# Two of four feature pairs of an FFN's opening tile in three passes of rounded parts, and two other PSUM banks for the output projection's last odd tiles

## The chip, the cores and the metric

The kernel runs on one core of a Trainium2 chip. A core has TensorE (PE in the profile; PEld is its weight load), VectorE (DVE), ScalarE (ACT), GpSimd (POOL) and SyncE (SP), each with a program of its own, and 16 DMA engines. Matmuls write to PSUM, which has eight banks; all else lies in SBUF. The metric is the device time of one execution in microseconds (us), as the median of several runs.

## What is computed

One step of a decoder trunk for 512 new prompt tokens and 8 sample tokens (520 columns in all), model width 1024, all in float32: a half-step SwiGLU FFN, a mixer (a causal pooling path and a Mamba-2 state space path side by side, with an output projection back to width 1024), a second half-step FFN, and a final norm.

```python
h = x
h = h + 0.5 * _swiglu(_rms_norm(h, ffn1_norm), ffn1_w_gate, ffn1_w_up, ffn1_w_down)
m, p, c, s = _hybrid_mixer(_rms_norm(h, mix_norm), st_pool, st_conv, st_ssm, start_pos, w_in, ..., w_out)
h = h + m
h = h + 0.5 * _swiglu(_rms_norm(h, ffn2_norm), ffn2_w_gate, ffn2_w_up, ffn2_w_down)
y = _rms_norm(h, final_norm)

def _swiglu(x, wg, wu, wd):
    return (jax.nn.silu(x @ wg) * (x @ wu)) @ wd
```

## The kernel before

Activations lie with the features on the 128 partitions and the 520 tokens in the columns, so h is eight blocks (d = 0 to 7) of 128x520. The columns are worked in two halves of 260 (b = 0, 1; HB is 260), so that the result of a matmul fits a bank.

**Numbers in two parts.** Most matmuls don't take float32 operands. A value is split into a rounded part (hi, of the type float32r, made by ACT with a cast) and the rest (lo, made by DVE as value minus hi; some weights get theirs by a DMA that adds). A product of two such pairs takes three matmuls: hi x hi, hi x lo and lo x hi. mm3 (L150 to L155) issues these three in a row; mm_low_last (L157 to L165) issues the two with the high weight for all four blocks of features and then the four with the low weight. On the rows of the profile L151, L154, L155, L160 and L165 are these matmuls. A matmul with plain float32 operands is one instruction in the code and two records in the profile; L311 is the line of such.

**The FFN in tiles.** The hidden width of 2816 is 22 tiles (f = 0 to 21) of 128. Gate and up weights of a tile come by two DMAs of 512 KB into a raw buffer; there are two such pairs of buffers. Except for the opening tile, a tile is computed by seven products instead of eight: the four blocks gate/up by column half, with features in two halves, are combined by sums of weights (tile names s, room, then shi/slo for the parts) and sums of activations. These activations are the seven slots of xth (high parts) and xtl (low parts): for each pair j of feature blocks (j and j + 4), slots 0 to 2 are the values themselves (xg, scaled by the norm's weights, with four places: slots 0 to 2 and a fourth that has no slot of its own), slots 3 to 6 are sums of them (xd, by the three steps of sums4). prep_pair makes all this for one pair: three DVE sums, two ACT casts (128x780 and 128x1040) and two DVE subtractions. Products 1 and 6 of a tile accumulate in a bank of the tag A, one after the other in the same bank with an ACT copy between them (L504); the others in a pair of banks of the tag BE.

**The opening tile.** Tile 0 of the second FFN is computed with plain float32 matmuls instead, eight for each pair j, 32 in all, straight from xg and the raw weights (plain, L298 to L315), so that PE has work while DVE and ACT make the parts for the tiles behind. Its results gather in two pairs of BE banks, P_00 (gate) and P_01 (up), which ACT copies out (keep).

**The end of the mixer.** The output projection has three groups of input features (j = 0, 1, 2; wout). A call wout(j, d2) loads a weight of 512 KB, splits it, and does four tiles of twelve matmuls: d = 2 d2 and 2 d2 + 1, for both halves. DVE adds each tile to h from its bank (L1311). In the last group (j = 2), fin follows on each block of h: ACT squares it (sq), DVE adds the squares up (acc) for the norm, and ACT writes the block of xg for pair j once d is 4 or more (the order of groups below says when). This last group and the opening tile are interleaved by

```python
LAST_PLAN = "h0 h2 h1 n0 h3 n1 n2 n3"
```

where h0 to h3 are the four calls of the last group and n0 to n3 the calls fill(0) to fill(3), one for each pair of the opening tile. For j = 2, the tiles of the last group take their banks from the two of the tag ps, and those of d = 1 from the two of the tag A.

The order of instructions on an engine isn't that of the code: when the program is built, a scheduler with a model of durations orders each engine's instructions, except where the code pins them or names one behind which another must be issued (keep_in_program_order, issue_after, high_priority). On the chip each engine runs its list in that order and waits at semaphores.

**Raw buffers.** The buffers of the projection's weights and of FFN tiles are the same ones, so a load of FFN weights waits until the DVE subtraction that reads the buffer last is done. Tile 2's weights go to tile 1's buffers, tile 3's to tile 0's.

Of the kernel before, what the change touches and what calls it, by code (L numbers as in the profile page):

```python
# [10 lines left out]
F32 = mybir.dt.float32  # L11
# [6 lines left out]
P = 128  # L18
# [50 lines left out]
def tile_trunk_step(ctx: ExitStack, tc: tile.TileContext, ins: dict, outs: dict):  # L69
# [97 lines left out]
    def ws(w, k, m=P):  # L167
        return w[:, k * m : (k + 1) * m]
# [86 lines left out]
    def prep_pair(nx, cell, xg, j, name, late=None):  # L255
        xth, xtl, _, _ = nx
        xd = cell(f"xd_{name}{j}")
        last = sums4(xg, xd)

        def parts(s, t):  # L260
            return part(xth[:, j, t], xtl[:, j, t], s)

        parts(xg[:, 0:3], slice(0, 3))
        if late is not None:
            late.append(lambda: parts(xd, slice(3, 7)))
            return None
        return last.ins, *parts(xd, slice(3, 7))

    Down = namedtuple("Down", "c d")

    class Ffn:
# [15 lines left out]
        def plain_load(self, f, j=None, us=(0, 1), queue=nc.sync):  # L287
# [3 lines left out]
            for u in us:  # L291
# [4 lines left out]
                     for t in (self.raw[f][:, u], src[2 * f + u]))  # L296
                queue.dma_start(out=next(q), in_=next(q))

        def plain(self, f, xg, j, us=(0, 1), pin=False):
            for u in us:  # L300
                if (f, u) not in self.banks:
                    n = f"P{self.i}_{f}{u}"
                    if f == 1 and u == 0:
                        bs = [ps[0].tile([P, 512], F32, tag="A", bufs=2, name=f"{n}{b}") for b in range(2)]
                    else:
                        t = ps[0].tile([P, 2, 512], F32, tag="BE", bufs=2, name=n)
                        bs = [t[:, 0], t[:, 1], t]
                    self.banks[f, u] = bs
                for q in range(2):
                    for b, slot in enumerate(((0, 1), (3, 2))):  # L310
                        mm = nc.tensor.matmul(self.banks[f, u][b][:, :HB], ws(self.raw[f][:, u], j + 4 * q),  # L311
                                              xg[:, slot[q]], start=j == q == 0, stop=j == 3 and q == 1,
                                              skip_group_check=True)
                        if pin and q == b == 0:
                            tc.keep_in_program_order(mm)  # L315

        def keep(self, f, us):

# [463 lines left out]
    def fin(d, b, hs):  # L782
# [5 lines left out]
        if j >= 0 and b:  # L788
            f2[j] = scaled(cell2, "ffn2_norm", j, "f2")

    def fill(j):
        if not j:
            f2["ffn"].plain_load(0)
        f2["ffn"].plain(0, f2[j], j)
        last = j == KD // 2 - 1
        if last:
            with tc.high_priority():
                f2["ffn"].keep(0, (0,))
        f2["ends"] = prep_pair(f2["ffn"].nx, cell2, f2[j], j, "f2")
        if last:  # L800
            with tc.high_priority(), tc.issue_after(f2["ends"][1]):
                f2["copied"] = f2["ffn"].keep(0, (1,))
# [95 lines left out]
def mixer(tc, ins, outs, e):  # L898
# [393 lines left out]
    def wout(cat, j, d2, fin=None):  # L1292
# [8 lines left out]
                               else behind.get((j, d2), ()))  # L1301
        for d in (2 * d2, 2 * d2 + 1):
            for b, hs in enumerate(HALVES):
                if d != 1 or j != 2:
                    ps = bank(f"wo{j}_{d}{b}")
                else:
                    ps = e["ps"][0].tile([P, 512], F32, tag="A", bufs=2, name=f"wo{j}_{d}{b}")
                i = range((d % 2) * 4, (d % 2) * 4 + 4)
                mm_low_last(ps[:, :HB], *([ws(w, k) for k in i] for w in (wh, wl)),
                            *([cat[:, q, k, hs] for k in range(4)] for q in range(2)), True)  # L1310
                rows.append(nc.vector.tensor_tensor(out=h[:, d, hs], in0=ps[:, :HB], in1=h[:, d, hs], op=ALU.add).ins)  # L1311
                if fin is not None:
                    fin(d, b, hs)
# [179 lines left out]
```

## Time and profile before

| | us |
|---|---|
| median of 3 runs | 950.68 |
| lowest, highest | 949.75, 951.92 |
| the profiled execution's own time | 952.73 |
| its span, first to last instruction | 950.9 |

The page gives the busy time of each engine over the span and in 40 slices, the chain of work that ended last, and the costliest groups of instructions. Windows give busy times of a stretch; the timeline gives rows with start, duration, engine, line, operation, out<-in and count, and in brackets the engine's idle time ahead of it with what ended it. In this trace the out projection's last group and the opening tile lie between 576 and 614 us, and tile 1 of the second FFN up to about 624 us. Columns 128x260 are one half's width.

### The profile page before, as it was taken

The page shows a single profiled execution, that of the slowest core. Times are in us where ns is not written, and L with a number is a line of the kernel's source. Part 1 is how long each engine was busy: PE and PEld are TensorE (multiplying, and loading weights), DVE is VectorE, ACT ScalarE, POOL GpSimd, SP SyncE. Part 2 cuts the span into 40 slices and gives each one's busy share as a digit, 9 for nine tenths or more (in the row PEclk, how much of TensorE's full clock was granted, in tenths as well). Part 3 has the DMA queues.
Part 4 walks back from the last instruction along what each step waited for, and adds up shares of the span by engine and source line. Part 5 has one row for each costly group of instructions (what it writes and reads, how often), then busy time and mean ns, then how long its engine had stood idle before and what let it go on. Part 6 is the DMA issues. An engine that isn't in the chain of part 4 may idle for free. (4 is left out here: it accounts for less than half of the span.)

```text
span 950.9 us, 19685 instructions
## 1 busy us (share of the span) xinstructions
PE 941.6 (99%) x7674; PEld 923.9 (97%) x7674; DVE 851.8 (90%) x1462; ACT 635.7 (67%) x1178; POOL 152.6 (16%) x230
## 2 busy tenths in 40 slices
PE   9999999999999999999999999999999999999996
PEld 8999999999999999999999899999999999999996
DVE  6899899998988698779998998999999999999986
ACT  7777756667566465475768745777776677766764
POOL 0011100100100002146251100111112101122120
PEclk9999999999999999999999999999999999999998
DMA  7666554455553335354364443546666655767642
GB/s 212 180 164 146 148 147 140 113 135 164 134 153 97 87 96 162 91 169 150 97 179 133 140 113 117 139 120 156 164 178 175 164 147 137 172 203 181 171 158 91
DMA packets 54123, 138.36 MB, mean 146 GB/s; under 512 B 7878, under 2 KB 16006, under 8 KB 54030
## 3 DMA queue, kind: packets, MB, share of 16 engines
q1 hardware_dynamic: 40046, 104.20, 34.6%
q0 software_dynamic: 13712, 32.78, 18.6%
q8 instruction: 60, 0.98, 0.4%
q14 instruction: 33, 0.27, 0.1%
q10 hardware_dynamic: 272, 0.13, 0.0%
HBM read 129.74 MB, written 7.34 MB: 144 GB/s over the span
## 5 line engine op out<-in xcount | busy, mean ns | idle before, releaser
L504 ACT COPY ac<-A 128x260 f32<-128x260 f32 x85 | 31.7, 373 | 34.6 <-PE A L165 16.4
L433 DVE TENSOR_TENSOR s<-raw 128x1024 f32<-128x1024 f32 x39 | 47.6, 1221 | 4.0 <-DMA raw<-in_w2gu 2.5
L504 ACT COPY ac<-BE 128x260 f32<-128x260 f32 x41 | 15.5, 377 | 33.4 <-PE BE L165 17.6
L151 PE MATMUL inx<-xh_mx,whi_inx 128*128 128x260 f32 x112 | 31.8, 284 | 0.0
L154 PE MATMUL inx<-xl_mx,whi_inx 128*128 128x260 f32 x112 | 31.6, 282 | 0.0
L155 PE MATMUL inx<-xh_mx,wlo_inx 128*128 128x260 f32 x112 | 31.6, 282 | 0.0
L1033 DVE SCALAR_TENSOR_TENSOR A<-U,h,A 128x544 f32<-128x544 f32 x36 | 28.4, 789 | 1.8 <-ACT A L1031 1.4
L311 PE MATMUL P<-x,raw 128*128 128x260 f32 x128 | 29.3, 390 | 0.0
L311 PEld LDWEIGHTS P<-x,raw 128*128 128x128 f32 x128 | 24.9, 196 | 3.9
L160 PE MATMUL wo<-catg,whi_wo 128*128 128x260 f32 x192 | 27.4, 285 | 0.0
L160 PEld LDWEIGHTS wo<-catg,whi_wo 128*128 128x128 f32 x192 | 24.8, 188 | 0.2
L139 ACT CAST thi<-raw 128x1024 fp32r<-128x1024 f32 (+1 forms) x14 | 14.2, 1014 | 15.5 <-PE wo L160 4.8
L1311 DVE TENSOR_TENSOR h<-wo,h 128x260 f32<-128x260 f32 x48 | 19.2, 423 | 4.9 <-PE wo L165 4.7
L1199 ACT ACTIVATE so<-br,sxdt 128x128 f32<-128x128 f32 x64 | 22.7, 375 | 1.2 <-DVE room L1201 0.7
L252 DVE TENSOR_TENSOR gs<-gq,gs 128x780 fp32r<-128x780 f32 (+1 forms) x28 | 23.2, 829 | 0.0
L151 PE MATMUL inz<-xh_mx,whi_inz 128*128 128x260 f32 x80 | 22.9, 287 | 0.0
L154 PE MATMUL inz<-xl_mx,whi_inz 128*128 128x260 f32 x80 | 22.7, 283 | 0.0
L155 PE MATMUL inz<-xh_mx,wlo_inz 128*128 128x260 f32 x80 | 22.6, 283 | 0.0
L512 DVE TENSOR_TENSOR BE<-BE,ac 128x260 f32<-128x260 f32 (+1 forms) x41 | 18.5, 451 | 3.1 <-PE BE L155 1.7
L151 PEld LDWEIGHTS inx<-xh_mx,whi_inx 128*128 128x128 f32 x112 | 21.1, 188 | 0.2 <-issue 0.2
L160 PE MATMUL A<-xth_f,qs 128*128 128x260 f32 x84 | 21.2, 283 | 0.0
L160 PE MATMUL A<-xtl_f,qs 128*128 128x260 f32 x84 | 21.2, 284 | 0.0
(3135 smaller groups left out, 4380.9 us busy)
## 6 DMA issues: line engine op xcount, KB each, us to landing
raw<-in_w2gu SPq DMA_DIRECT2D x44, 512.0 KB, 4.3
raw<-in_w1gu SPq DMA_DIRECT2D x41, 512.0 KB, 4.2
raw<-in_w_in SPq DMA_DIRECT2D x24, 512.0 KB, 3.6
raw<-in_w1d SPq DMA_DIRECT2D x16, 512.0 KB, 4.6
raw<-in_w2d SPq DMA_DIRECT2D x16, 512.0 KB, 4.3
raw<-in_w_out SPq DMA_DIRECT2D x12, 512.0 KB, 3.5
ab<-scr_acs SPq DMA_DIRECT2D x8, 512.0 KB, 6.3
h<-in_state_ssm SPq DMA_DIRECT2D x16, 256.0 KB, 3.7
```

What stands on the lines that cost most here:

```text
L151: first = nc.tensor.matmul(ps, whi, xhi, start=start, stop=False, **kw)
L154: nc.tensor.matmul(ps, whi, xlo, start=False, stop=False, **kw)
L155: nc.tensor.matmul(ps, wlo, xhi, start=False, stop=stop, **kw)
L160: mm = nc.tensor.matmul(ps, w, x, start=start, stop=False, **kw)
L252: low = nc.vector.tensor_tensor(out=lo, in0=s, in1=hi.bitcast(F32), op=ALU.subtract)
L311: mm = nc.tensor.matmul(self.banks[f, u][b][:, :HB], ws(self.raw[f][:, u], j + 4 * q), xg[:, slot[q]], start=j == q == 0, stop=j == 3 and ...
L433: nc.vector.tensor_tensor(out=s1, in0=diag, in1=up0, op=ALU.add)
L504: self.copied = nc.scalar.copy(keep, out[:, :HB]).ins
L512: nc.vector.tensor_tensor(out=be[:, s], in0=be[:, s], in1=a[:, s], op=ALU.add)
L1033: nc.vector.scalar_tensor_tensor(out=A[:, :n], in0=U[:, j : j + n], scalar=w(j), in1=A[:, :n], op0=ALU.mult, op1=ALU.add)
L1199: nc.scalar.activation(out=o[:, q], in_=br, func=AF.Copy, scale=sxdt[:, j, b : b + 1]))
L1311: rows.append(nc.vector.tensor_tensor(out=h[:, d, hs], in0=ps[:, :HB], in1=h[:, d, hs], op=ALU.add).ins)
```

## The change

There are two edits. In the first, pairs 0 and 1 of the opening tile are no longer multiplied in plain float32. weight_parts splits the weights of these pairs (a 128x1024 piece of the raw buffer) into w0h and w0l, and parts_plain multiplies them in three passes by mm3: the activations of slots 0 to 2 are the parts that xth and xtl hold anyway, and the fourth place gets parts of its own, x3h and x3l (128x260 each, once for each of the two pairs, from a pool of two buffers). Since these parts are needed, prep_pair now comes ahead of the matmuls of pairs 0 and 1. Pairs 2 and 3 stay as they were. In the second edit, all odd tiles of the projection's last group take the banks of the tag A, not those of d = 1 alone.

```diff
-        parts(xg[:, 0:3], slice(0, 3))
+        first = parts(xg[:, 0:3], slice(0, 3))
...
-        return last.ins, *parts(xd, slice(3, 7))
+        return last.ins, *parts(xd, slice(3, 7)), *first
...
+        def parts_plain(self, f, w, x3, j):
+            self.plain_banks(f, (0, 1))
+            for u in range(2):
+                for q in range(2):
+                    wh, wl = (t[:, 2 * u + q, j * P : j * P + P] for t in w)
+                    for b, slot in enumerate(((0, 1), (3, 2))):
+                        xh, xl = x3 if slot[q] == 3 else (t[:, j, slot[q]] for t in self.nx[:2])
+                        mm3(self.banks[f, u][b][:, :HB], wh, wl, xh, xl, j == q == 0, False, skip_group_check=True)
...
+    def weight_parts(cast, low):
+        src = f2["ffn"].raw[0].rearrange("p u (q c) -> p (u q) c", q=2)[:, :, : 2 * P]
+        hi, lo = (f2["xg"].tile([P, 4, 2 * P], F32R, tag=t, name=t) for t in ("w0h", "w0l"))
+        with queued(cast):
+            nc.scalar.copy(hi, src)
+        with queued(low):
+            nc.vector.tensor_tensor(out=lo, in0=src, in1=hi.bitcast(F32), op=ALU.subtract)
+        f2["w0"] = hi, lo
+
     def fill(j):
+        ffn, last = f2["ffn"], j == KD // 2 - 1
         if not j:
-            f2["ffn"].plain_load(0)
-        f2["ffn"].plain(0, f2[j], j)
-        last = j == KD // 2 - 1
+            ffn.plain_load(0)
+        if j < 2:
+            ends = prep_pair(ffn.nx, cell2, f2[j], j, "f2")
+            if not j:
+                weight_parts(*ends[3:])
+            x3 = [tmp.tile([P, HB], F32R, tag="ta", name=f"{t}{j}") for t in ("x3h", "x3l")]
+            part(*x3, f2[j][:, 3])
+            ffn.parts_plain(0, f2["w0"], x3, j)
+            return
+        ffn.plain(0, f2[j], j)
         if last:
             with tc.high_priority():
-                f2["ffn"].keep(0, (0,))
-        f2["ends"] = prep_pair(f2["ffn"].nx, cell2, f2[j], j, "f2")
+                ffn.keep(0, (0,))
+        f2["ends"] = prep_pair(ffn.nx, cell2, f2[j], j, "f2")
...
-                if d != 1 or j != 2:
+                if d % 2 == 0 or j != 2:
                     ps = bank(f"wo{j}_{d}{b}")
                 else:
                     ps = e["ps"][0].tile([P, 512], F32, tag="A", bufs=2, name=f"wo{j}_{d}{b}")
```

The change also moves instructions, since the scheduler orders the new program afresh. Up to the tile wo_41 of the last group PE's list is the same, and from tile 2's first product on it is the same again.

On PE, behind wo_41 (wo_dh is the projection's tile of block d and half h; P_00 and P_01 are the opening tile's gate and up), there stood before:

```order
L311 MATMUL P_00_7451<-xg_f_7345,raw 128x260 x2
L311 MATMUL P_01_7456<-xg_f_7345,raw 128x260 x2
L160 MATMUL wo_50_7348<-catg_7093,thi 128x260 x8
L165 MATMUL wo_50_7348<-catg_7093,tlo 128x260 x4
L160 MATMUL wo_51_7362<-catg_7093,thi 128x260 x8
L165 MATMUL wo_51_7362<-catg_7093,tlo 128x260 x4
L311 MATMUL P_00_7451<-xg_f_7345,raw 128x260 x2
L311 MATMUL P_01_7456<-xg_f_7345,raw 128x260 x2
L311 MATMUL P_00_7451<-xg_f_7379,raw 128x260 x2
L311 MATMUL P_01_7456<-xg_f_7379,raw 128x260 x2
```

Now the tiles wo_50 to wo_31 follow one another there, and the first 24 matmuls in three passes stand behind wo_31. The start of that place:

```order
L160 MATMUL wo_31_7432<-catg_7093,whi_wo_7383 128x260 x8
L165 MATMUL wo_31_7432<-catg_7093,wlo_wo_7384 128x260 x4
L151 MATMUL P_00_7467<-xth_f_7242,w0h 128x260
L154 MATMUL P_00_7467<-xtl_f_7243,w0h 128x260
L151 MATMUL P_01_7468<-xth_f_7242,w0h 128x260
L154 MATMUL P_01_7468<-xtl_f_7243,w0h 128x260
L155 MATMUL P_00_7467<-xth_f_7242,w0l 128x260
L151 MATMUL P_00_7467<-x3h_7463,w0h 128x260
L154 MATMUL P_00_7467<-x3l_7464,w0h 128x260
L155 MATMUL P_00_7467<-x3h_7463,w0l 128x260
```

So twelve projection tiles run without a break, the other four between the first and the second block of three-pass matmuls, and the plain matmuls of pairs 2 and 3 behind both.

On DVE, from the sum s of tile 1's weights to the low part wlo_1a of its gate weights (L141 and L252 are subtractions for low parts), the list now begins so; w0l is new, and x3l (not shown) stands further up:

```order
L446 TENSOR_TENSOR s_2_1_7665<-raw 128x1024
L238 TENSOR_TENSOR xd_f_7451<-xg_f_7345 128x520
L1341 TENSOR_TENSOR h<-wo_51_7362,h 128x260
L252 TENSOR_TENSOR xtl_f_7243<-xg_f_7345,xth_f_7242 128x780
L448 TENSOR_TENSOR room<-s_2_1_7665,raw 128x512
L810 TENSOR_TENSOR w0l<-raw,w0h 128x1024
L1341 TENSOR_TENSOR h<-wo_20_7387,h 128x260
L240 SCALAR_TENSOR_TENSOR xd_f_7451<-xd_f_7451,xg_f_7345 128x260
L141 TENSOR_TENSOR slo_1c<-s_2_1_7665,shi_1c 128x1024
```

Behind these come, up to wlo_1a, three additions to h, the second room, one acc, one xd of 128x260 and one xtl of 128x780. Before, the xtl of pair 0's sums (128x1040), tile 1's slo_1d, a second acc and the first sum of pair 1 stood ahead of wlo_1a as well, and there was no w0l.

On ACT, at the end of the opening (sq is the square of a block of h for the norm, xg_f a scaled block, whi_2a the cast of tile 2's gate weights), there stood before:

```order
L203 ACTIVATE sq_f_6_7502<-h 128x520
L234 ACTIVATE xg_f_7505<-h 128x520
L251 CAST xth_f_7242<-xg_f_7505 128x780
L396 CAST whi_2a<-raw 128x1024
L397 ACTIVATE wlo_2a<-whi_2a 128x512
L203 ACTIVATE sq_f_7_7536<-h 128x520
L234 ACTIVATE xg_f_7539<-h 128x520
```

and there stands now:

```order
L409 CAST whi_2a<-raw 128x1024
L410 ACTIVATE wlo_2a<-whi_2a 128x512
L203 ACTIVATE sq_f_6_7526<-h 128x520
L234 ACTIVATE xg_f_7529<-h 128x520
L203 ACTIVATE sq_f_7_7560<-h 128x520
L234 ACTIVATE xg_f_7563<-h 128x520
L251 CAST xth_f_7242<-xg_f_7529 128x780
L251 CAST xth_f_7242<-xg_f_7563 128x780
```

The cast of tile 2's gate weights and its negation moved ahead of the square and the scaling of the last two blocks of h.

More of the change, by code (lines that the diff above doesn't have):

```diff
@@ L297, in plain_load, with plain_banks @@
                 queue.dma_start(out=next(q), in_=next(q))
-        def plain(self, f, xg, j, us=(0, 1), pin=False):
+        def parts_plain(self, f, w, x3, j):
[6 more added lines that the diff above has]
+                        mm3(self.banks[f, u][b][:, :HB], wh, wl, xh, xl, j == q == 0, False, skip_group_check=True)
+        def plain(self, f, xg, j, us=(0, 1), pin=False):
+            self.plain_banks(f, us)
+            for u in us:
+                for q in range(2):
+                    for b, slot in enumerate(((0, 1), (3, 2))):
+                        mm = nc.tensor.matmul(self.banks[f, u][b][:, :HB], ws(self.raw[f][:, u], j + 4 * q),
+                                              xg[:, slot[q]], start=j == q == 0, stop=j == 3 and q == 1,
+                                              skip_group_check=True)
+                        if pin and q == b == 0:
+                            tc.keep_in_program_order(mm)
+        def plain_banks(self, f, us):
             for u in us:
@@ L308, in plain @@
                     self.banks[f, u] = bs
[L309 to L315, printed above, removed]
         def keep(self, f, us):
```

## The prediction

> **What bounds the kernel now.** First the page: the span, the busy row and the clock row.
>
> ```profile
> span 950.9 us, 19685 instructions
> ...
> PE 941.6 (99%) x7674; PEld 923.9 (97%) x7674; DVE 851.8 (90%) x1462; ACT 635.7 (67%) x1178; POOL 152.6 (16%) x230
> ...
> PEclk9999999999999999999999999999999999999998
> ```
>
> TensorE (PE) is busy for all but 9 us and its clock is full, so a gain needs less PE work. Then the waits of PE over the whole span, longest first:
>
> ```profile
> PE warm L709 <- DVE eps L95: 1.1, 1, 1.1
> PE factor L870 <- PE psl L864: 0.6, 1, 0.6
> ```
>
> Both stand at the kernel's ends; no wait of PE is listed in the changed stretch. Two windows of that stretch (from the first tile of the out projection's last group to FFN tile 1's end):
>
> ```profile
> core 0: us, PE busy (x) PEld busy (x) DVE busy (x) ACT busy (x) POOL busy (x), PEclk, DMA share, GB/s
> 576.06:613.75 37.69, 37.69 (x265) 35.81 (x264) 32.30 (x54) 24.91 (x35) 4.99 (x6) 1.00 0.48 120
> 613.75:622.69 8.94, 8.94 (x71) 8.76 (x70) 8.91 (x10) 6.22 (x10) 0.00 (x0) 1.00 0.39 117
> ```
>
> PE never stops here. VectorE (DVE) has 5.4 us free in the first window and none in the second, though: whatever PE needs from DVE there is only just in time. I make the sum against this one execution (span 950.9 us, own time 952.73 us) and carry its difference to the median of 950.68 us.
>
> **What the three passes save on PE.** The plain float32 matmuls by the tile view, the last long run of them with the two rows behind it (start, duration), and 26 rows of three-pass form from the last stage, first and last:
>
> ```profile
> L311 PEld LDWEIGHTS P<-xg_f,raw x64: 187/190/190, 584.5 to 613.3; 128*128 128x128 f32 x64
> L311 PE MATMUL P<-xg_f,raw x64: 380/382/383, 584.7 to 613.5; 128*128 128x260 f32 x64
> ```
> ```profile
> 608.25 3.67 PE L311 MATMUL P<-xg_f,raw 128*128 128x260 f32 x16
> 611.56 0.48 PE L160 MATMUL A<-xth_f,whi_1a 128*128 128x260 f32 x1
> 611.88 0.28 PE L160 MATMUL A<-xtl_f,whi_1a 128*128 128x260 f32 x1
> ```
> ```profile
> 907.01 0.28 PE L154 MATMUL dh<-g,whi_2d 128*128 128x260 f32 x1
> ...
> 910.03 0.28 PE L155 MATMUL dh<-g,slo_2d 128*128 128x260 f32 x1
> ```
>
> A plain matmul leaves two records, so 64 records are the 32 matmuls of the opening tile. Eight of them (x16) take 3.31 us to the next start, and that next row takes 0.32 us to its successor where 0.12 is usual: 3.51 us, or 0.439 us each. In three-pass form 25 steps take 3.02 us, 0.121 each, 0.362 us for three. Half of the 32 change form: 16 x 0.077 = **1.23 us less PE work**, the most that the change can bring. By the Trainium skill ("FP8 and Floating Point Precision", TensorE Precision Notes) true float32 takes four passes through the array; at 0.121 us a pass the saving would be 16 x 0.121 = 1.94 us, an estimate that the 0.439 us above contradicts.
>
> **What is added, and its cover.** ScalarE (ACT) gets one 128x1024 cast (w0h) and two 128x260 copies (x3h), DVE one 128x1024 subtraction (w0l) and two of 128x260 (x3l). Rows that price these and the work around them, first DVE, then ACT; on either engine the next row starts 0.08 to 0.10 us before the end of the row ahead, if it waits for nothing:
>
> ```profile
> 613.10 0.42 DVE L242 SCALAR_TENSOR_TENSOR xd_f<-xd_f,xg_f 128x260 f32<-128x260 f32 x1
> 613.44 0.69 DVE L400 TENSOR_TENSOR wlo_2a<-raw,whi_2a 128x512 fp32r<-128x512 f32 x1
> 614.04 0.97 DVE L252 TENSOR_TENSOR xtl_f<-xg_f,xth_f 128x780 fp32r<-128x780 f32 x1
> 614.92 1.24 DVE L252 TENSOR_TENSOR xtl_f<-xd_f,xth_f 128x1040 fp32r<-128x1040 f32 x1
> 616.07 3.41 DVE L214 RECIPROCAL r_f<-r_f 128x260 f32<-128x260 f32 x2
> ...
> 620.74 1.22 DVE L141 TENSOR_TENSOR slo_2c<-s,shi_2c 128x1024 fp32r<-128x1024 f32 x1
> 621.87 0.68 DVE L436 TENSOR_TENSOR room<-room,raw 128x512 f32<-128x512 f32 x1
> ```
> ```profile
> 607.98 1.05 ACT L396 CAST whi_2a<-raw 128x1024 fp32r<-128x1024 f32 x1 [0.28 <-PE wo L160]
> ...
> 609.05 0.63 ACT L397 ACTIVATE wlo_2a<-whi_2a 128x512 fp32r<-128x512 f32 x1
> ...
> 609.59 0.62 ACT L203 ACTIVATE sq_f<-h 128x520 f32<-128x520 f32 x1
> ...
> 610.12 0.71 ACT L234 ACTIVATE xg_f<-h 128x520 f32<-128x520 f32 x1
> ...
> 613.56 1.06 ACT L251 CAST xth_f<-xd_f 128x1040 fp32r<-128x1040 f32 x1
> ...
> 614.52 0.59 ACT L324 COPY ac<-P 128x520 f32<-128x520 f32 x1
> 615.01 0.86 ACT L213 ACTIVATE r_f<-psr_f,eps 128x260 f32<-128x260 f32 x2
> 616.39 0.38 ACT L504 COPY ac<-A 128x260 f32<-128x260 f32 x1 [0.52 <-PE A L165]
> ```
>
> So DVE steps are 0.34 (260 columns), 0.60 (512 or 520), 0.88 (780), 1.15 (1040) and 1.13 us (1024). DVE gets 1.13 + 2 x 0.34 = 1.8 us more, ACT 0.95 + 2 x 0.28 = 1.5. The 5.4 us that DVE has free hide it in amount; whether it does in place has to be followed.
>
> **Place 1: the first three-pass block.** One wo tile of 12 matmuls by two starts, and the row with which DVE begins FFN tile 1:
>
> ```profile
> 576.06 1.12 PE L160 MATMUL wo<-catg,whi_wo 128*128 128x260 f32 x8
> 577.01 0.65 PE L165 MATMUL wo<-catg,wlo_wo 128*128 128x260 f32 x4
> 577.50 1.11 PE L160 MATMUL wo<-catg,whi_wo 128*128 128x260 f32 x8
> ```
> ```profile
> 587.36 1.23 DVE L433 TENSOR_TENSOR s<-raw 128x1024 f32<-128x1024 f32 x1 [0.67 <-DMA raw<-in_w2gu]
> ```
>
> A wo tile takes 1.44 us; twelve now stand in a row, so the block starts at 576.06 + 17.28 = 593.3. On DVE, s comes about 0.3 us later than now (x3h sits ahead of the cast whose low part frees the buffer that s's load waits for): 587.7. To w0l stand s, xd, h, xtl and room: 1.13 + 0.60 + 0.34 + 0.88 + 0.60, so w0l ends at 592.4, and the block's fifth matmul wants it at 593.8. Covered by 1.4 us; past that each us costs one. The bank edit belongs here: by the same count the evacuation of wo_51 ends near 589.8, and on two banks the tile two behind it would start at 589.0 and wait 0.8 us. On four it waits for tiles long evacuated. The edit is worth 0 now (PE shows no wait) and keeps a wait from coming; FFN tile 1 takes the bank of wo_70, free near 603, at 606.7. The second x3h reuses a buffer that the first block frees at 596.2, which ACT doesn't reach before 596.
>
> **Place 2: the end of the opening.** PE without waits: 593.3 + 24 x 0.121 = 596.2; four wo tiles, 602.0; second block, 604.9; plain 1.76, four of FFN tile 1 0.48, plain 1.76 and 1.76, the norm's two sums 0.88, plain 1.76: 613.3; 15 rows of tile 1 at 0.12: **615.1** for the first matmul of tile 1's second product in bank A (shi_1d). Before it stands at 616.92, with five more rows of tile 1 (0.60 us) ahead; 616.92 - 615.1 - 0.6 = 1.22, the saving again. It writes a bank that ACT must first have copied out, and this copy stands behind casts that wait for DVE. The chain has six links. The rows on which it hangs:
>
> ```profile
> 601.44 0.69 DVE L400 TENSOR_TENSOR wlo_1a<-raw,whi_1a 128x512 fp32r<-128x512 f32 x1
> ```
> ```profile
> 602.15 0.33 SPq L389 DMA_DIRECT2D raw<-in_w2gu  x1
> ```
> ```profile
> raw<-in_w2gu SPq DMA_DIRECT2D x1, 512.0 KB, 4.5
> ```
> ```profile
> DMA to landing us min/median/max: 3.4/3.6/7.0
> ```
> ```profile
> s<-in_w2gu POOLq DMA_DIRECT2D x1, 512.0 KB, 6.4
> ```
> ```profile
> 616.92 0.29 PE L160 MATMUL A<-xth_f,shi_1d 128*128 128x260 f32 x1
> ```
>
> 1. wlo_1a: from s (587.7) stand three rows of 1024, four of 512 to 520, two of 780 and seven of 260 ahead of it: 3.39 + 2.40 + 1.76 + 2.38 = 9.9, so it runs from 597.6 to 598.3 (now to 602.13).
> 2. Its end lets SyncE load tile 2's gate half, as at 602.15 now. At 4.5 us it lands at 602.8.
> 3. ACT now has the cast of that half and its negation ahead of the square of h6 (order below the change): 602.8 + 1.07 + 0.54 puts the square at 604.4, though h6 is ready at 598.2 + 0.60 + 1.13 + 2 x 0.34 + 1.15 + 0.42 = 602.2 (DVE's rows behind wlo_1a). DVE idles about 1.1 us for it.
> 4. Square, scale, square, scale (0.53 + 0.62 + 0.53 + 0.62), then the cast xth of pair 2, 0.84: 607.6.
> 5. DVE: 0.88 + 0.60 + 0.88 + 1.15 + 0.34 + 0.60 + 0.42 to the end of pair 2's last sum: 612.5.
> 6. ACT: two casts 0.96 each, a copy 0.49, the roots 0.76, the copy of A 0.38: 616.1.
>
> So PE waits 1.0 us of the 1.2 us saved, and passes this point 0.2 us earlier than now. Behind it nothing differs: DVE reaches the reciprocals at 612.4 + 2 x 0.34 + 0.60 + 2 x 1.15 = 616.0 (now 616.07), and PE's rows from tile 2 on are the same, without waits. Every link but the load is a row of this trace; the load's bounds are 3.4 and 7.0 us. I take 4.5, the same load now, because in both orders the 6.4 us adding load of GpSimd runs beside it. **Forecast: 952.73 - 0.2 = 952.5 for an execution like the one shown, 950.5 us as a median.**
>
> **The rivals.** A, the wait doesn't come: every us by which the load lands sooner shortens it by one, and at the median of 3.6 us only 0.1 is left. For it: this load starts four us sooner, perhaps ahead of the adding load's traffic. Time 950.68 - 1.1 = 949.6. B, slower: the load lands as late as the adding load does, at 6.4 us. Chain and wait grow by 1.9: 950.68 - 0.2 + 1.9 = 952.4; from 4.7 us on, the change loses. For it: all of the load lies inside the adding one, where now only part does. Against it: 4.5 us with such a neighbour. C, the three passes aren't cheaper: 48 weight loads stand for 32, each 0.19 us, 16 x 0.19 = 3.0 us more, 953.7 if loads bound PE. Against it: 71 rows in the window of 8.94 us, 0.126 us each beside loads of 0.19, so the loads overlap. The Trainium skill ("Perfetto Trace Analysis", Identifying the Most-Contended Engine) gives the busy share of weight loads as a good measure of TensorE, which speaks against this change; the 0.126 us rows speak against the rule here. D, the change saves nothing on PE and PE arrives just as the copy is done: 950.7.
>
> **How the numbers follow.** Forecast 0.48, A 0.25, B 0.20, C 0.03, D 0.04. The range goes from A less 0.5 us (the spread of a median: three runs lie between 949.75 and 951.92) to B: 949.0 to 952.4. About 0.2%, 1.9 us, is what a measurement of this kernel can tell from no change. Below 948.8 lies only what spread adds to A: 0.05. Above 952.6 lie C and some of B: 0.10. Within: 0.85.
>
> **What would show it.** Right: blocks on w0h with steps of 0.121 us and no PE wait ahead of them; no wait on evacuation in the run of twelve wo tiles; whi_2a waiting for its load on ACT; a PE wait of about 1 us in FFN tile 1 for the copy of A; tile 2's first matmul near 622.5 (now 622.69). Wrong: a step above 0.13, a wait on w0l, a load of tile 2 that lands in under 4 or over 5.5 us, or a wait of PE behind tile 2.

## The result, and the profile after

The change makes the kernel slower: 953.49 us against 951.45 us for the kernel before on the same chip (medians of 15 runs each), a ratio of 1.0023 with a 95% interval of 1.0012 to 1.0033, or 1.1 to 3.1 us. Two further measurements of the same kernel, below, give 1.0022 and 1.0019. The forecast was 950.5 us, 0.2 us faster than before, with a range of 949.0 to 952.4 us.

The profiled execution of the changed kernel took 952.75 us, in the lower third of its 15 runs (951.78 to 958.59). Its page, the same three rows as in the prediction:

```profile
span 951.0 us, 19730 instructions
...
PE 940.8 (99%) x7690; PEld 923.3 (97%) x7690; DVE 852.5 (90%) x1465; ACT 637.4 (67%) x1181; POOL 151.9 (16%) x230
...
PEclk9999999999999999999999999999999999999998
```

PE does 0.8 us less work (941.6 before), and yet the span is as long. Among the longest waits of PE over the whole span, two rows were not there before (the first is two waits, one in FFN tile 1 and one in tile 3):

```profile
PE A L160 <- ACT ac L517: 0.8, 2, 0.5
...
PE BE_Down(c=0, d=0)_8690 L160 <- ACT BE_Down(c=0, d=0)_8690 L517: 0.5, 1, 0.5
```

The second lies 75 us behind the change. Two windows of this execution cut the program at tile 2's first matmul: from the mixer's last norm sums (psr_y, a place that all kernels here share, ahead of all that the change touches) to there, the **opening** from here on, and from there to PE's last row. Then the same two of the kernel before:

```profile
562.55:621.32 58.77, 58.25 (x451) 56.59 (x449) 54.00 (x83) 37.51 (x55) 5.01 (x6) 1.00 0.41 108
621.32:943.99 322.67, 320.97 (x2680) 320.12 (x2679) 298.32 (x519) 228.77 (x426) 55.10 (x81) 1.00 0.60 160
```
```profile
563.72:622.69 58.97, 58.97 (x434) 56.79 (x433) 52.76 (x80) 36.48 (x52) 4.99 (x6) 1.00 0.41 108
622.69:944.12 321.43, 320.53 (x2680) 320.04 (x2679) 299.08 (x519) 228.00 (x426) 55.05 (x81) 1.00 0.62 161
```

The first column behind the window is its length. The opening came out as forecast in this execution, 0.20 us shorter (why this is luck in part is said further down). The rest, which was to be the same, is 1.24 us longer. The execution shown before reached the opening 1.17 us later than this one (563.72 for 562.55, in a part of the program that the change leaves alone), which hides the loss when the two spans are compared.

### The profile page after: what moved, and what is told of

It is laid out like the page before. It is cut to its first block, busy times and chain, and to the rows that moved or that the text cites. A ratio compares the mean times of both kernels' runs of the same rounds, so it can differ in the third digit from the quotient of the medians.

```text
span 951.0 us, 19730 instructions
## 1 busy us (share of the span) xinstructions
PE 940.8 (99%) x7690; PEld 923.3 (97%) x7690; DVE 852.5 (90%) x1465; ACT 637.4 (67%) x1181; POOL 151.9 (16%) x230
## 5 line engine op out<-in xcount | busy, mean ns | idle before, releaser
L252 DVE TENSOR_TENSOR gs<-gq,gs 128x780 fp32r<-128x780 f32 (+1 forms) x28 | 23.2, 829 | 0.0
L251 ACT CAST gs<-gq 128x780 fp32r<-128x780 f32 (+1 forms) x28 | 20.6, 736 | 1.4 <-DVE gq L568 1.0
```

The lines of the kernel that those rows point to most:

```text
L251: cast = nc.scalar.copy(hi, s)
L252: low = nc.vector.tensor_tensor(out=lo, in0=s, in1=hi.bitcast(F32), op=ALU.subtract)
```

## Where the loss sits

**Behind the opening, place one: tile 3.** The timeline of before, DVE's rows around tile 2's and 3's parts and then ACT's (start, duration, engine, line, output and input):

```profile
625.17 0.69 DVE L529 TENSOR_TENSOR gq<-BE,r_f 128x520 f32<-128x520 f32 x1
625.77 1.22 DVE L141 TENSOR_TENSOR slo_2d<-room,shi_2d 128x1024 fp32r<-128x1024 f32 x1
626.91 1.22 DVE L141 TENSOR_TENSOR wlo_3a<-raw,whi_3a 128x1024 fp32r<-128x1024 f32 x1
```
```profile
626.54 0.62 ACT L535 ACTIVATE gq<-gq 128x520 f32<-128x520 f32 x1
628.64 0.38 ACT L504 COPY ac<-BE 128x260 f32<-128x260 f32 x1 [1.48 <-PE BE L165]
628.91 0.85 ACT L251 CAST gs<-gq 128x780 fp32r<-128x780 f32 x1
...
633.47 0.37 ACT L504 COPY ac<-A 128x260 f32<-128x260 f32 x1
```

and of the changed kernel, DVE, ACT, and the row of PE that waits:

```profile
623.90 1.22 DVE L141 TENSOR_TENSOR slo_2d<-room,shi_2d 128x1024 fp32r<-128x1024 f32 x1
625.04 1.22 DVE L141 TENSOR_TENSOR wlo_3a<-raw,whi_3a 128x1024 fp32r<-128x1024 f32 x1
626.17 0.69 DVE L542 TENSOR_TENSOR gq<-BE,r_f 128x520 f32<-128x520 f32 x1
```
```profile
627.52 0.64 ACT L548 ACTIVATE gq<-gq 128x520 f32<-128x520 f32 x1
...
629.66 1.05 ACT L139 CAST shi_3c<-s 128x1024 fp32r<-128x1024 f32 x1 [0.59 <-PE BE L160]
630.61 0.84 ACT L251 CAST gs<-gq 128x780 fp32r<-128x780 f32 x1
...
631.88 1.04 ACT L139 CAST shi_3d<-room 128x1024 fp32r<-128x1024 f32 x1
632.83 0.36 ACT L517 COPY ac<-A 128x260 f32<-128x260 f32 x1
```
```profile
632.35 0.64 PE L165 MATMUL A<-xth_f,wlo_3a 128*128 128x260 f32 x4
633.25 0.39 PE L160 MATMUL A<-xth_f,qs 128*128 128x260 f32 x1 [0.26 <-ACT ac L517]
633.47 0.28 PE L160 MATMUL A<-xtl_f,qs 128*128 128x260 f32 x1
```

The program order differs. Tile 1's gate product (gq, 0.69 us) stood ahead of slo_2d and wlo_3a on DVE and now stands behind both. Counted from tile 2's first matmul it runs 2.4 us later (625.17 - 622.69 = 2.48; 626.17 - 621.32 = 4.85). So ACT's Silu of it (gq<-gq) comes later, the cast gs of it falls behind shi_3c, and from shi_3c on four casts instead of three stand ahead of the copy of A for which PE waits: the copy starts 11.51 us behind tile 2's first matmul instead of 10.78, and PE wants it done at 11.51. From tile 3's first matmul to tile 4's takes 10.62 us for 10.07.

The loss is larger than the 0.26 us that the profile calls a wait. Four matmuls of 0.12 us a step would put the next start at 632.83; it comes at 633.25, and the step behind it is 0.22 us instead of 0.12. Together that is 0.52 us, 0.26 more than the idle time, which is counted only from the end of the row ahead. The same holds for the other waits of PE below.

**Place two: the first Down tile.** The timeline there, changed kernel and then before:

```profile
694.58 1.05 ACT L410 ACTIVATE wlo_Down(c=0, d=1)a<-whi_Down(c=0, d=1)a 128x1024 fp32r<-128x1024 f32 x1
695.54 0.37 ACT L517 COPY BE_Down(c=0, d=0)_8690<-A_Down(c=0, d=0)_8689 128x260 f32<-128x260 f32 x1
...
695.96 0.39 PE L160 MATMUL BE_Down(c=0, d=0)_8690<-gs,shi_Down(c=0, d=0)c 128*128 128x260 f32 x1 [0.50 <-ACT BE_Down(c=0, d=0)_8690 L517]
```
```profile
695.24 0.36 ACT L504 COPY BE_Down(c=0, d=0)_8646<-A_Down(c=0, d=0)_8645 128x260 f32<-128x260 f32 x1
695.51 1.06 ACT L397 ACTIVATE wlo_Down(c=0, d=1)a<-whi_Down(c=0, d=1)a 128x1024 fp32r<-128x1024 f32 x1
```

The negation of the next tile's weights (1.05 us, which nobody is waiting for) overtook a copy of 0.37 us for which PE waits. The stretch from this tile's first matmul to the next one's takes 10.79 us for 10.03.

**The opening, in other executions.** Five profiled executions have the change's opening row for row at full clock: the one above, two repeats (e_after2, e_after3) and two experiments that alter only later rows (e_old_order, e_gate). Beside each the time that tile 2's gate half took from issue to landing (the view of DMA issues):

| execution | landing | opening |
|---|---|---|
| before, twice | 4.5 in the first | 58.97, 58.96 |
| change | 4.2 | 58.77 |
| e_after2 | 4.3 | 58.98 |
| e_after3 | 4.6 | 59.17 |
| e_old_order | 4.9 | 59.49 |
| e_gate | 5.4 | 59.95 |

The opening grows one for one with the landing: 1.2 us more landing, 1.18 us more opening. The rows of the longest, e_gate (the timeline, and the row of the load in the view of DMA issues):

```profile
596.02 0.33 SPq L402 DMA_DIRECT2D raw<-in_w2gu  x1
...
601.46 1.05 ACT L409 CAST whi_2a<-raw 128x1024 fp32r<-128x1024 f32 x1 [4.52 <-DMA raw<-in_w2gu]
...
613.75 0.39 PE L160 MATMUL BE<-xtl_f,shi_1c 128*128 128x260 f32 x1 [1.08 <-DVE xtl_f L252]
...
614.75 0.39 PE L160 MATMUL A<-xth_f,shi_1d 128*128 128x260 f32 x1 [0.49 <-ACT ac L517]
```
```profile
raw<-in_w2gu SPq DMA_DIRECT2D x1, 512.0 KB, 5.4
```

ACT sits idle 4.52 us for the load, with the squares and scales of the last two blocks of h behind it, and PE then waits in two places for what hangs on them. The second wait, for the copy of A, is 0.49 to 0.50 us in all five; the first, for xtl_f, grows with the landing from less than the profile lists (at 4.2) through 0.3, 0.5 and 0.7 to 1.1 us.

## The experiments

Four theories are named in the expectations: "order" (ACT and DVE stand in another order behind the opening), "load" (the opening waits for tile 2's load), "weight loads" and "banks" (the three passes, or the use of the A banks, cost more in themselves than the trace makes them). Times are medians beside the median of before on the same chip, with the ratio and its 95% interval.

**One edit alone.** e_banks is before with the second edit, e_parts the change without it:

```diff
-                if d != 1 or j != 2:
+                if d % 2 == 0 or j != 2:
```

> The kernel before with the bank edit alone: all odd output tiles of the last group in the two A banks, the opening tile wholly in plain float32. ACT's and DVE's order in FFN tiles 2 to 21 becomes that of the full change; PE keeps its 32 plain matmuls. Theory 'order' (the time is lost behind the opening, because the bank edit reorders ACT and DVE there and PE then waits for copies and casts): slower than before by 1.5 to 3.5 us, since the same late order stands without the 1.2 us of saved PE work. Theory 'load' (the time is lost in the opening, where tile 2's weights land late in most executions and DVE's chain is longer by the three passes' work): within 0.7 us of before. Theory 'weight loads' (three passes are dearer than the trace makes them): within 0.7 us.

> The three-pass edit alone, with the bank rule of before (only tile 1 of the last group in an A bank). ACT's and DVE's order from FFN tile 2 on is that of before; in the opening PE may wait for the evacuation of an output tile, 0.8 us by the prediction's count. Theory 'order': no loss behind the opening, so between 1 us faster than before and the same (0.2 us gained in the opening, or up to 1.2 if the wait for the copy of A does not come). Theory 'load' or 'weight loads': slower than before by 1.5 to 2.5 us, as the full change is, or more by the evacuation wait.

e_banks: 953.39 for 951.12, 1.0031 (1.0019 to 1.0043, five runs). e_parts: 951.60 for 951.12, 1.0005 (0.9997 to 1.0014). So the edit that was priced at nothing makes a loss of this size, and the three passes alone make no difference that this can tell. In the order of the programs, e_parts has ACT's and DVE's rows of before from tile 2's gate rows on, and e_banks nearly those of the change: tile 1's gate product stands one row late there, behind slo_2d but not behind wlo_3a. e_parts has an opening of 59.01 us: it saves the work and gives it back in waits, most of it for two evacuations (in its list of PE's waits), which cost 1.0 us by the steps between PE's starts:

```profile
PE wo L160 <- DVE h L1341: 0.5, 2, 0.3
```

**Two of the odd tiles in the A banks.** e_parts15 is the change with this:

```diff
-                if d % 2 == 0 or j != 2:
+                if d not in (1, 5) or j != 2:
```

> The three-pass edit with output tiles 1 and 5 (not 3 and 7) in the A banks: the opening has one evacuation wait less than with tile 1 alone, and ACT's and DVE's order from FFN tile 2 on is that of before. Theory 'order': as fast as the three-pass edit alone or up to 0.8 us faster, 0.2 to 1.2 us faster than before. Theory 'load' or 'weight loads': slower than before by 1.5 to 2.5 us.

953.02 for 951.12, 1.0019 (1.0010 to 1.0027). The expectation of theory "order" missed: the order from tile 2 on is that of before, and it is slow all the same. Its opening took 60.12 us, 1.15 more than before, and the list of PE's waits names the place (the step between PE's starts there is 1.51 us for 0.12):

```profile
PE P L155 <- DVE w0l L810: 1.2, 1, 1.2
```

Here the scheduler moved the first three-pass block ahead of two projection tiles, 2.9 us sooner, and w0l's cover of 1.4 us, as the prediction counted it, was gone.

**The changed kernel again.** e_after2 and e_after3 are unaltered.

> The changed kernel once more, unaltered, on the same chip as the two halves, for a second profiled execution. All theories: 1.1 to 3.2 us slower than before (ratio 1.0012 to 1.0033). Theory 'order': in this execution too PE loses 1 us or more against before between tile 2's first matmul and the end, in tiles 3 to 9, behind ACT's copies of A and BE. Theory 'load': the loss against before is there already at tile 2's first matmul. If it is scatter, the places where PE loses differ from those of the first execution.

> The changed kernel once more, on the chip of the three others, for a third profiled execution. All theories: 1.1 to 3.2 us slower than before. Theory 'order': tile 3's to tile 4's first matmul 10.5 to 10.7 us and Down tile (0,0)'s to (0,1)'s 10.7 to 11.0 us again, while other stretches differ between executions.

952.96 for 951.12, 1.0022 (1.0014 to 1.0031), and 953.04 for 951.33, 1.0019 (1.0009 to 1.0028). The two places repeat (table below); the opening differs by its load.

**The kernel before again.** e_before2 is the kernel before, unaltered:

> The kernel before, unaltered, for a second profiled execution. If the first one was late by chance in the mixer, its sums of the norm (psr_y) start 1 to 2 us earlier than the 563.72 us of the first; from there to tile 2's first matmul 58.7 to 59.2 us, and from there to PE's last row 320.9 to 321.9 us, without a wait of PE.

The norm sums start at 562.27 (563.72 in the first), the opening takes 58.96 us, so the first execution of before was late in the mixer by chance. The rest takes 323.88 us here and not the 320.9 to 321.9 expected, with waits in later Down tiles: 2.4 us of scatter in a kernel without any change.

**Seven of eight half tiles in the A banks,** once with the later order of before (e_seven_old) and once with that of the change (e_seven_new, which has (1, 0) for (5, 1) here):

```diff
-                if d % 2 == 0 or j != 2:
+                if d % 2 == 0 or j != 2 or (d, b) == (5, 1):
```

> The changed kernel with one of the eight half tiles (tile 5's second half) kept in the other banks: seven of eight use the A banks. From 20 rows behind FFN tile 1's last copy on, ACT's and DVE's order is row for row that of before. Theory 'order' (the loss of about 2 us sits behind the opening and comes with the other ACT and DVE order): from tile 2's first matmul to PE's last row 320.9 to 321.6 us as before (321.4), and the whole within 0.8 us of before. Theory 'banks' (the loss comes from using the A banks, whatever the order): the same stretch 322.5 or more, the whole 1.5 to 2.5 us slower than before.

> The changed kernel with another one of the eight half tiles (tile 1's first half) kept in the other banks: seven of eight use the A banks here too, but from 20 rows behind FFN tile 1's last copy on ACT's and DVE's order is row for row that of the changed kernel. Theory 'order': the stretch from tile 2's first matmul to PE's last row 322.5 or more, the whole 1.5 us or more slower than the other kernel with seven. Theory 'banks': as the other kernel with seven, within 0.7 us.

953.28 for 951.70, 1.0016 (1.0008 to 1.0025), and 956.65, 1.0053 (1.0040 to 1.0066). The two places go with the order (10.06 and 10.03 us in the first, 10.58 and 11.19 in the second), against theory "banks". By the letter of the expectations the first came out as theory "banks" has it: the stretch behind the opening took 323.05 us and the whole was 1.6 us slower. But neither can decide: that stretch took 323.88 us in e_before2, without any change, and the whole times hold the openings, which changed too, to 60.56 and 61.45 us. e_gate below separates banks and order with the opening kept. In the second the load landed after 6.2 us, and PE waited behind it:

```profile
PE A L160 <- ACT xth_f L251: 2.6, 1, 2.6
```

**Two rows put back by hand.** e_pin issues the cast shi_3d behind A_2's last copy and the negation behind the Down tile's copy:

```diff
-                    nc.scalar.activation(out=lo[:, n2:], ..., scale=-1.0)
+                    with queued(*((self.copies[Down(0, 0), 1],) if (i, f) == (2, (0, 1)) else ())):
+                        nc.scalar.activation(out=lo[:, n2:], ..., scale=-1.0)
...
-            e2 = split(s2, 1024, f"{n}d", wx, 2, ("shi", "slo"))
+            with queued(*((self.copies[2, 7],) if (i, f) == (2, 3) else ())):
+                e2 = split(s2, 1024, f"{n}d", wx, 2, ("shi", "slo"))
```

> The changed kernel with two rows of ACT put back behind the copies that they had overtaken: the cast shi_3d behind the last copy of A_2, and the negation wlo_Down(c=0,d=1)a behind Down tile (0,0)'s copy of A. The scheduler answers by other orders in some later places, neither before's nor the change's. Theory 'order': PE's waits at these two places (0.26 and 0.5 us in the profiled execution of the change) are gone, and the whole is 0.4 to 1 us faster than the changed kernel, if the later places are no worse. Theory 'banks': as the changed kernel.

952.32 for 951.70, 1.0006 (0.9997 to 1.0015). The Down place is healed (10.02 us). Tile 3 isn't (10.66): the copy of A comes in time there, but shi_3d now delays the next copy (BE<-A, two rows behind it) and slo_3d, and PE loses some 0.3 us at each instead. The cause stands further up, in the gate product, as e_gate shows.

**The negation alone.** e_old_order has the first of these two edits and not the second.

> The changed kernel with one edge more: the negation wlo_Down(c=0,d=1)a is issued behind Down tile (0,0)'s copy of A. The scheduler answers with ACT's and DVE's order of before from FFN tile 2 on, row for row; PE's order, the banks, and ACT's and DVE's order in the opening are those of the change. Theory 'order': the stretches that lost in all executions with the new order come back (tile 3's to tile 4's first matmul 10.07 us for 10.6, Down tile (0,0)'s to (0,1)'s 10.03 for 10.8), so 1.3 us faster than the changed kernel on the same chip or more, and within 0.7 us of before. Theory 'banks': as the changed kernel, within 0.5 us. Theory 'load' (the opening alone, where tile 2's weights land late): as the changed kernel.

952.43 for 951.33, 1.0007 (0.9998 to 1.0016). The expectation states the order wrongly: in the trace, tile 1's gate product still stands behind slo_2d and wlo_3a, as in the change. So it tests one place: that one is back (10.03 us), tile 3 stays at 10.62.

**The gate product alone.** e_gate puts one edge on DVE, and everything from that row on falls into the order of before:

```diff
-            e2 = split(s2, 1024, f"{n}d", wx, 2, ("shi", "slo"))
+            e2 = split(s2, 1024, f"{n}d", wx, 2, ("shi", "slo"), (self.gated,) if (i, f) == (2, 2) else ())
...
-            nc.vector.tensor_tensor(out=self.tg[f], in0=be, ..., op=ALU.mult)
+            self.gated = nc.vector.tensor_tensor(out=self.tg[f], in0=be, ..., op=ALU.mult).ins
```

> The changed kernel with one edge on DVE: slo_2d is issued behind tile 1's gate product (gq<-BE). PE's order, the banks and the whole opening are those of the change; from that row on ACT's and DVE's order is that of before, at tile 3 as well. Theory 'order': tile 3's to tile 4's first matmul 10.07 us for 10.6 and Down tile (0,0)'s to (0,1)'s 10.03 for 10.8, so 0.8 to 2 us faster than the change (1.0019 to 1.0023 of before), within 1.2 us of before, with the opening's 58.8 to 59.5 us kept. Theory 'banks' (the A banks in the last group cost the time whatever the order): as the change.

952.21 for 951.55, 1.0007 (0.9998 to 1.0016). The timeline of DVE at the place, to be set beside those of before and the change above:

```profile
623.95 0.69 DVE L542 TENSOR_TENSOR gq<-BE,r_f 128x520 f32<-128x520 f32 x1
624.56 1.22 DVE L141 TENSOR_TENSOR slo_2d<-room,shi_2d 128x1024 fp32r<-128x1024 f32 x1
625.69 1.22 DVE L141 TENSOR_TENSOR wlo_3a<-raw,whi_3a 128x1024 fp32r<-128x1024 f32 x1
```

PE's program, the banks and the opening's rows are the change's, behind them ACT's and DVE's rows are those of before, and both places are back. Of the whole time some 1.3 us of the loss is gone by the medians (1.0007 for the 1.0019 to 1.0023 of the change); the intervals overlap, so the two places show the cause and not this figure. The opening took 59.95 us and not the 58.8 to 59.5 expected, with the load at 5.4 us.

**The cast moved.** e_cast_later issues whi_2a behind the opening's last scale and leaves the later order of the change:

```diff
-                nc.scalar.activation(out=out[:, s], in_=hd[:, s], func=AF.Copy, scale=v(norm, d))
+                last_scale[:] = [nc.scalar.activation(out=out[:, s], in_=hd[:, s], func=AF.Copy, scale=v(norm, d)).ins]
...
-        f2["ffn"].behind[2] = (f2["ends"][0],), (f2["ffn"].plain_out(0),), True
+        f2["ffn"].behind[2] = (f2["ends"][0], *last_scale), (f2["ffn"].plain_out(0),), True
```

> The changed kernel with tile 2's cast whi_2a issued behind the last scale of the opening (h6 and h7), so that ACT no longer waits for the load ahead of them; the order from FFN tile 2 on is the new one. By the prediction's links 2 and 3 the square of h6 starts about 1.1 us earlier, and PE's wait of about 1 us for the copy of A in FFN tile 1 goes: from the norm's sums of the mixer to tile 2's first matmul 57.8 to 58.3 us (58.8 and 59.0 in the change), whatever the load takes. Theory 'order': the whole 0.5 to 1.2 us faster than the changed kernel, 0.8 to 1.5 us slower than before still. Theory 'load' (the opening makes the whole loss, in executions in which the load lands late): as fast as before or faster.

951.31 for 951.33, 1.0001 (0.9991 to 1.0011), 1.7 us faster than the change on the same chip. Its opening in the windows, one window:

```profile
561.06:618.95 57.89, 57.89 (x450) 56.53 (x449) 53.72 (x83) 37.53 (x55) 5.02 (x6) 1.00 0.40 107
```

PE is busy throughout. Against 58.97 us that is 1.08 us less: the saving that the change was made of, of which the prediction's count is 1.23. The scheduler also put two DVE rows of the opening in other places, an xd ahead of an xtl and an xtl ahead of wlo_2a, so not the cast alone has moved. The whole time is what theory "load" expected, and 0.5 us faster than theory "order" allowed; but both places behind the opening still take 10.62 and 10.83 us, so the opening doesn't make the whole loss: its saving offsets theirs within the interval.

**Both.** e_both has the moved cast, the gate edge and the negation's edge; e_gate_cast has the moved cast and gets the later order of before by another edge in the opening (weight_parts(ends[3], ends[0]) for weight_parts(*ends[3:])).

> The changed kernel with whi_2a behind the last scale, slo_2d behind tile 1's gate product on DVE, and the negation wlo_Down(c=0,d=1)a behind Down tile (0,0)'s copy of A. ACT's order from tile 2 on differs from that of before in 4 places, none of them at tile 3 or Down tile (0,0). Theory 'order': both gains at once, 1.5 to 2.7 us faster than the changed kernel, 0 to 1 us faster than before. Theory 'banks': 0.5 to 1.2 us faster than the changed kernel.

> The changed kernel with whi_2a behind the opening's last scale and w0l behind pair 0's last sum; from 20 rows behind FFN tile 1's last copy on ACT's and DVE's order is that of before. Theory 'order' with the load's wait: both losses gone, opening 57.8 to 58.3 us and the two places at 10.07 and 10.03, 2 to 3.5 us faster than the change and 0.5 to 1.5 us faster than before. If the two parts don't add up: no faster than before.

e_both: 950.41 for 951.33, 0.9984 (0.9975 to 0.9994). e_gate_cast: 950.67 for 951.55, 0.9990 (0.9981 to 0.9999). Both beat the kernel before, by 0.6 to 2.4 and 0.1 to 1.8 us, and the change by 2.6 to 3.3 us (medians and ratios). Within the spread the two parts add up: some 1.3 from the order and 1.7 from the cast. The windows of e_both:

```profile
563.34:621.19 57.85, 57.85 (x450) 56.50 (x449) 53.68 (x82) 37.50 (x55) 5.01 (x6) 1.00 0.42 109
621.19:943.16 321.97, 320.87 (x2680) 320.05 (x2679) 297.92 (x520) 228.09 (x426) 54.94 (x81) 1.00 0.62 160
```

e_both and e_cast_later have the same opening row for row; tile 2's load landed after 5.1 us in the one and 3.6 in the other, and the openings are 57.85 and 57.89: with the cast behind the scales, the load decides nothing in this range. In e_gate_cast, whose three-pass blocks stand in another order, it landed after 7.6 us, and the opening is 58.38.

All profiled executions by stretch, in us; each is a difference of two starts on PE's timeline (opening; tile 3's to tile 4's first matmul; Down tile (0,0)'s to (0,1)'s; and all else from tile 2's first matmul to PE's last row):

| kernel | opening | tile 3 | Down (0,0) | all else |
|---|---|---|---|---|
| before | 58.97 | 10.07 | 10.03 | 301.33 |
| e_before2 | 58.96 | 10.07 | 10.02 | 303.79 |
| e_parts | 59.01 | 10.06 | 10.03 | 301.00 |
| e_parts15 | 60.12 | 10.07 | 10.03 | 302.06 |
| e_seven_old | 60.56 | 10.06 | 10.03 | 302.96 |
| change | 58.77 | 10.62 | 10.79 | 301.26 |
| e_after2 | 58.98 | 10.59 | 10.85 | 302.31 |
| e_after3 | 59.17 | 10.62 | 10.83 | 301.24 |
| e_banks | 58.82 | 10.16 | 11.03 | 305.22 |
| e_seven_new | 61.45 | 10.58 | 11.19 | 301.34 |
| e_pin | 61.27 | 10.66 | 10.02 | 302.15 |
| e_old_order | 59.49 | 10.62 | 10.03 | 301.52 |
| e_cast_later | 57.89 | 10.62 | 10.83 | 301.77 |
| e_gate | 59.95 | 10.06 | 10.03 | 302.12 |
| e_both | 57.85 | 10.06 | 10.02 | 301.89 |
| e_gate_cast | 58.38 | 10.07 | 10.03 | 301.87 |

The two middle columns go by the order: 10.06 to 10.07 and 10.02 to 10.03 us where it is that of before at this place, 10.6 and 10.8 to 11.2 where it is that of the change; e_banks loses at tile 2 (10.82 for 10.08 us) what the others lose at tile 3. The opening of e_pin holds some 1.3 us of a lower clock (last section; 61.27 us for the 59.95 of e_gate, with nearly the same landing). The last column scatters by 2.8 us, e_banks apart, and shows no loss with the order of the change; this is why a single pair of spans says nothing about a change of 2 us.

## Why the prediction was wrong, step by step

**The failed step** is the sentence "Behind it nothing differs", and with it "The edit is worth 0 now". PE's list from tile 2 on is indeed the same, but ACT's and DVE's are not: with the three passes in place, the bank edit has the scheduler put tile 1's gate product two rows later (the change beside e_parts), and other rows behind it. Two of these moves cost PE 0.54 and 0.79 us on average of the three executions of the change, and nearly the same in each. The prediction looked at when DVE reaches the reciprocals and at PE's own rows, and took "without waits" from the trace of before, where these two waits are absent because of an order that the change no longer has. e_gate shows this: one DVE row put back, and both places are as before.

**The mis-sized terms** are two, both in the opening. One is the load: the forecast used 4.5 us; the five openings have 4.2 to 5.4, 4.7 on average. The other is what a wait costs beyond its length. The prediction counts five more rows of tile 1 behind this point of PE, 0.60 us, and five there are; but two steps behind the wait take 0.23 us instead of 0.12. The last row of the stretch before (its first, at 616.92, stands in the prediction), and the rows of the change:

```profile
622.69 0.28 PE L160 MATMUL A<-xth_f,whi_2a 128*128 128x260 f32 x1
```
```profile
614.71 0.39 PE L160 MATMUL A<-xth_f,shi_1d 128*128 128x260 f32 x1 [0.49 <-ACT ac L517]
614.94 0.28 PE L160 MATMUL A<-xtl_f,shi_1d 128*128 128x260 f32 x1
...
616.89 0.39 PE L160 MATMUL BE<-xth_f,shi_1d 128*128 128x260 f32 x1
617.12 0.28 PE L160 MATMUL BE<-xtl_f,shi_1d 128*128 128x260 f32 x1
...
621.32 0.28 PE L160 MATMUL A<-xth_f,whi_2a 128*128 128x260 f32 x1
```

From shi_1d's first matmul to tile 2's it is 5.77 us before and 6.61 in the change, 0.84 more and not 0.60. So at a landing of 4.5 us the prediction's own chain gains nothing. In the execution shown the load landed 0.3 us sooner than assumed and this term took 0.24 us back: that its opening is 0.20 us shorter, as forecast to a tenth, is luck in part. On average the five openings take 59.27 us, 0.3 slower than before instead of 0.2 faster.

Link 2 and its slope were right (one for one). Rival B named this mechanism and put the point from which the change loses at 4.7 us; the rows put it near 4.3. Its 6.4 us was reached by no execution of the change; at this place other programs had 6.2 (e_seven_new) and 7.6 (e_gate_cast). e_cast_later shows the rest: with ACT's wait gone the opening is 1.1 us shorter than before.

**Together**: 0.3 + 0.54 + 0.79 = 1.6 us of the 1.7 to 2.0 us that the three medians show. The rest, within the intervals, is not assigned, and the 0.3 rests on five executions.

**The saving on PE** was nearly right: 1.08 to 1.12 us for the 1.23 counted. Three passes aren't limited by their weight loads (against rival C: the change's first block does 24 matmuls in 2.87 us, 0.12 each), and the saving is there (against D). **The wait in tile 1** came, and the execution shown lost 0.88 us by its waits there (58.77 us for the 57.89 of e_cast_later) where 1.0 was forecast. But the path was only half right: the forecast has PE wait for the copy of A alone, and what grows with the load is the wait ahead of it, for xtl_f. Both stand behind the same two casts of ACT. **The twelve projection tiles** ran without a wait for an evacuation in the change; without the bank edit e_parts has two, 1.0 us in all by the steps where one of 0.8 was counted. **w0l** was covered in the change; in e_parts15 the block stands 2.9 us sooner, 1.5 past the cover, and PE loses 1.5 us there, which is the price as stated. **The marker** that was named, "a wait of PE behind tile 2", is what the profile shows.

## What to carry to other kernels

When a scheduler orders the program, compare the order on every engine to the end of the kernel, not only around the edit, and check each row that PE waits for: a copy of 0.37 us overtaken by a row of 1 us that nobody needs yet is a loss, even far from the edit. An engine in order that waits for a load holds up everything behind it, so a cast that waits for a DMA belongs behind short work that is ready and on the path. And before calling a change bad, look whether its gain and its loss are in different places: here two or three ordering edges turned 0.2% slower into 0.1 to 0.2% faster.

## What was not expected of the hardware

The same 512 KB load took 3.6 to 7.6 us from issue to landing at this place of the program (e_cast_later and e_gate_cast), so one trace's landing time says little about the next: of the change's five openings, four were no shorter than before.

In e_pin the granted clock of TensorE (1.00 is full) fell to half for some 3 us, right behind waits of PE of 1.08 and 0.49 us. Windows of 1 us (length, PE busy, PEld, DVE, ACT, POOL, granted clock, DMA share, GB/s):

```profile
613.00:614.00 1.00, 0.06 (x1) 0.06 (x1) 1.00 (x2) 1.00 (x3) 0.00 (x0) 1.00 0.93 365
...
616.00:617.00 1.00, 1.00 (x7) 1.00 (x6) 1.00 (x2) 0.00 (x0) 0.00 (x0) 0.50 0.00 0
617.00:618.00 1.00, 1.00 (x6) 1.00 (x6) 1.00 (x1) 0.38 (x1) 0.00 (x0) 0.50 0.00 0
618.00:619.00 1.00, 1.00 (x7) 1.00 (x6) 0.97 (x2) 0.38 (x1) 0.00 (x0) 0.50 0.00 0
619.00:620.00 1.00, 1.00 (x9) 1.00 (x9) 0.70 (x2) 0.21 (x1) 0.00 (x0) 0.82 0.00 0
```

PE's timeline of the same execution, four matmuls and the start behind them:

```profile
616.07 1.07 PE L165 MATMUL BE<-xth_f,slo_1c 128*128 128x260 f32 x4
616.94 0.42 PE L160 MATMUL A<-xtl_f,shi_1d 128*128 128x260 f32 x1
```

They take 0.87 us to the next start, and 0.48 elsewhere. The longer steps last from about 616.0 to 619.3 us. e_gate waited as long at the same place and kept its clock at 1.00. The Trainium skill ("TensorE: Matmul & The Clock Gate", What's actually happening) states a free-running window of about 3.4 us: after an idle window TensorE is set to half rate, after a busy one to full. The length of this dip agrees with it, but the idle time here was 1.6 us, less than half a window. So a wait of PE can be followed by a loss of the clock, here of 1.3 us; how often it is was not measured, and that the waits were the cause is not shown.
